# Moving the beginnings of the weight tiles by 16 to 240 bytes in a decoder trunk

## The chip, the cores and the metric

The kernel runs on one core of a Trainium2 chip. The metric is the device time of one execution in microseconds; several executions are timed, and one more is taken by the hardware profiler, whose records are read below.

## What is computed

A causal trunk of two decoder layers on 512 tokens of width 1024, in fp32. Layer 0 mixes tokens by multi-scale retention (4 heads), layer 1 by forgetting attention (16 heads). All is laid out with features on partitions and tokens along the columns.

```python
for i in range(DEPTH):                                   # 2 layers
    h = h + 0.5 * swiglu(rmsnorm(h, nw[0]), ffn_w_in[i, 0], ffn_w_out[i, 0])   # 1024 -> 2 x 2816 -> 1024
    hn = rmsnorm(h, nw[1])
    h = h + (retention(hn, ...) if i % 2 == 0 else forgetting_attention(hn, ...))
    h = h + 0.5 * swiglu(rmsnorm(h, nw[2]), ffn_w_in[i, 1], ffn_w_out[i, 1])
    gate = jax.nn.sigmoid(rmsnorm(h, nw[3]) @ ple_w_gate[i])
    h = h + gate * (p[i] @ ple_w_proj[i])
return rmsnorm(h, final_norm_w)
```

## The kernel before

Every product is made with fp32r operands that are split in two: a high part (the value rounded to fp32r) and a low part (the rest). Three matmuls stand for one: high x high, high x low, low x high (`mm3`, L310 to L314). A matmul takes 128 x 128 weights, which TensorE loads before it (PEld in the profile), and a moving operand of 128 rows and 128, 256 or 512 columns.

**Moving operands.** The activations lie in *units*, tiles of 128 x 512 fp32 (2,048 bytes a partition), in the pools `ua`, `ub`, `uc` and `ud`. A matmul moves a whole unit (512 columns) or a half (256).

**Weights.** The class `Weights` brings every weight tile in the order of a list, `W.plan`, two tiles ahead of use. `load` starts a DMA of 128 x 1024 fp32 into a `wraw` tile on SyncE's queue; `split` (L82, L83) lets ScalarE write the high part and VectorE or GpSimd the low part into a tile of the name `w8`, 128 x 2 x 1024, which the profile calls `w`; `negated` (L120 to L122) makes the low part with ScalarE and an adding DMA from GpSimd's queue. `w8` tiles come from `wpool`, three in turn; in the last stage from `wkept` with five, and two more of its weight tiles are put into units of `ub`. Three functions make a `w8` tile: `chunk`, `emit_parts` (the first two tiles of the program) and `first` (a `Pair`).

**Where the tiles meet which columns.**

- The four FFNs. Two blocks of the 22 are made in a plain way (`plain`, L524, 256 columns, 96 matmuls a block). The other 20 are *pairs* in a Strassen-like scheme: `product` (L493) makes 12 matmuls of 256 columns, and a pair has seven such products, two with the `w8` tile (`pair.t`), five with sums of the quarters of the weights, which VectorE adds up (L151) and which lie in tiles `s12`, `s34` and `a12` (`s` and `a` in the profile) of a pool that is opened for one FFN. So 24 of 84 matmuls of a pair have `w8` weights.
- The FFNs' second matrix (`out_blocks`, L312 to L314): 512 columns, in three parts of 6, 8 and 8 blocks of the activations. In each part the first two of the eight output blocks are made in turn, three matmuls with the one tile, three with the other.
- The projections of both mixers, the output projections and the first gated embedding (`proj`, `out_part`, `OutBoth`, `ple`): 512 columns, L312 to L314. In `v_part` (L678 to L680) it is the other way round: units are the weights, and the `w8` tile moves with 512 columns.
- The last gated embedding works on two halves of the tokens: 256 columns, L312 to L314.

**Where the tiles lie.** The pools follow one another along each partition. The units, `wraw` and `wpool` hold tiles whose lengths are multiples of 2,048 bytes, so all units and all `w8` tiles of `wpool` begin at the same place modulo 256. The distance of a tile from this place, modulo 256, is called its *beginning* here: 0 for units and these `w8` tiles. Every piece of weights within a tile lies a multiple of 512 bytes behind its start, so it has the tile's beginning. The pool `stat` behind them holds six small tiles that take 32 bytes each, and so whatever pool is opened later begins 192 bytes further: the tiles `s12`, `s34`, `a12` and the five of `wkept` have the beginning 192.

The order of TensorE's instructions is written by hand (`manual_schedule`); the other engines run in the order of issue.

Of the kernel before, what the change touches and what calls it, by code (L numbers as in the profile page):

```python
# [12 lines left out]
F32R = mybir.dt.float32r  # L13
# [4 lines left out]
P = 128  # L18
# [7 lines left out]
RH = 4  # L26
FH = 16
LOOKAHEAD = 2
KEPT = 7
PLAIN = (2, 2, 2, 2)  # L30
CHUNKS = [((0, 6), (6, 14), (14, 22)) for n in PLAIN]
# [4 lines left out]
class Pair:  # L36
# [3 lines left out]
    def __init__(self, ffn, q, r):  # L40
        self.ffn, self.q, self.r, self.direct = ffn, q, r, False
# [13 lines left out]
class Weights:  # L55
# [3 lines left out]
    def __init__(self, tc, raw_pool, pool):  # L59
        self.tc, self.nc, self.raw_pool, self.pool = tc, tc.nc, raw_pool, pool  # L60
        self.plan, self.ready, self.used = [], [], 0
        self.low = self.nc.vector
        self.limit, self.spare = None, []
        self.sum_pool, self.open_ffn, self.pairs_used = None, None, 0
        self.ahead, self.behind = 0, ()

    def emit(self, upto):
        while len(self.ready) < min(upto, self.limit):
            src = self.plan[len(self.ready)]
            self.ready.append(self.first(src) if isinstance(src, Pair) else self.chunk(src))  # L70
            self.emit_sums()

    def load(self, src):
        raw = self.raw_pool.tile([P, 1024], F32, name="wraw")
        self.nc.sync.dma_start(out=raw[:, : src.shape[1]], in_=src)
        return raw

    def split(self, raw, hi, lo, src=None):
        if self.low is None and src is not None:
            self.negated(raw, hi, lo, src)  # L80
            return
        self.nc.scalar.copy(hi, raw)  # L82
        self.low.tensor_tensor(out=lo, in0=raw, in1=hi.bitcast(F32), op=ALU.subtract)  # L83

    def chunk(self, src):
        n = src.shape[1]
        raw = self.load(src)
        if self.spare:
            tiles = [self.spare.pop(0)() for _ in range(4)]
            for i in range(2):  # L90
                self.split(raw[:, 512 * i : 512 * (i + 1)], tiles[i], tiles[2 + i])
            return Halves(tiles[0:2]), Halves(tiles[2:4])
        t = self.pool.tile([P, 2, 1024], F32R, name="w8")
        self.split(raw[:, :n], t[:, 0, :n], t[:, 1, :n], src)
        return t[:, 0, :], t[:, 1, :]

    def emit_parts(self, parts):

        nc = self.nc
        halves = lambda ap: ap.rearrange("p (h c) -> p h c", h=2)  # L100
        tiles = [
            (
                self.raw_pool.tile([P, 1024], F32, name="wraw"),
                self.pool.tile([P, 2, 1024], F32R, name="w8"),
            )
            for _ in range(2)
        ]
        for j0, j1 in parts:
            cs = slice(j0 * P, j1 * P)
            for src, (raw, t) in zip(self.plan, tiles):  # L110
                r, hi, lo = (halves(x)[:, :, cs] for x in (raw, t[:, 0, :], t[:, 1, :]))
                nc.sync.dma_start(out=r, in_=halves(src)[:, :, cs])
                nc.vector.tensor_copy(hi, r)
                nc.vector.tensor_tensor(out=lo, in0=r, in1=hi.bitcast(F32), op=ALU.subtract)
            yield
        self.ready += [(t[:, 0, :], t[:, 1, :]) for _, t in tiles]
# [7 lines left out]
    def first(self, pair):  # L124

        pair.raw = self.load(pair.q)
        pair.t = self.pool.tile([P, 2, 1024], F32R, name="w8")
        hi, lo = pair.t[:, 0, :], pair.t[:, 1, :]
        if pair.direct:
            self.split(pair.raw, hi, lo)  # L130
        else:
            self.negated(pair.raw, hi, lo, pair.q)
# [41 lines left out]
    def take(self, src):  # L174
        assert self.plan[self.used] is src
        self.emit(self.used + 1 + LOOKAHEAD)
        self.used += 1
# [10 lines left out]
def trunk(ctx, tc, a):  # L188
# [9 lines left out]
    wraw = ctx.enter_context(tc.tile_pool(name="wraw", bufs=4))  # L198
    wpool = ctx.enter_context(tc.tile_pool(name="wpool", bufs=LOOKAHEAD + 1))
    tmp = ctx.enter_context(tc.tile_pool(name="tmp", bufs=7))  # L200
# [4 lines left out]
    W = Weights(tc, wraw, wpool)  # L205

    def unit(pool):
        return pool.tile([P, S], F32R, name="unit_" + {id(ua): "a", id(ub): "b", id(uc): "c", id(ud): "d"}[id(pool)])


    ffn_src = []
    for i in range(4):
        ins = [Pair(i, a["ffn_w_in"][i, m, 0], a["ffn_w_in"][i, m, 1]) for m in range(NF)]
# [12 lines left out]
    ple_g = [[a["ple_gate"][l, m] for m in range(KB)] for l in range(2)]  # L226
    ple_p = [[a["ple_proj"][l, c] for c in range(2)] for l in range(2)]
# [11 lines left out]
    def plan_ple(l):  # L239
        W.plan += [ple_p[l][0]] + ple_g[l][0:5] + [ple_p[l][1]] + ple_g[l][5:8]  # L240
# [22 lines left out]
    plan_ffn(3)  # L263
    plan_ple(1)
    W.limit = len(W.plan) - KEPT


    hall = hpool.tile([P, KB, S], F32, name="hall")
# [42 lines left out]
    def mm3(out, wh, wl, xh, xl, first, last):  # L311
        nc.tensor.matmul(out, wh, xh, start=first, stop=False)  # L312
        nc.tensor.matmul(out, wh, xl, start=False, stop=False)  # L313
        nc.tensor.matmul(out, wl, xh, start=False, stop=last)  # L314
# [749 lines left out]
    def ple(l, n, nxt, phi, plo, parts=1):  # L1064

        w = S // parts
        with ExitStack() as pools:
            if parts > 1:
                W.emit(W.limit)
                W.pool = pools.enter_context(tc.tile_pool(name="wkept", bufs=KEPT - 2, reuse_waits="tile"))  # L1070
                W.spare = [lambda: unit(ub)] * 8
# [120 lines left out]
    norms[2].extra = ud  # L1192
    first = W.emit_parts(((0, 1), (1, 2), (2, 4)))
    next(first)
    load_x(1, 2)
    load_x(2, 4)
# [15 lines left out]
    def ffn_ple(i, l, n, mid, nxt, stack, apool, parts):  # L1212
        phi, plo = [], []

        def load():
            pv = a["pT"][l].rearrange("(b p) t -> b p t", p=P)
            for b in range(2):
                t1 = temp()
                nc.sync.dma_start(out=t1, in_=pv[b])
                phi.append(unit(uc))  # L1220
                plo.append(unit(uc))
                split(t1, phi[b], plo[b])

        ffn(i, n, mid, stack, apool, load)
        stack = open_ffn(i + 1) if i < 3 else None
        ple(l, mid, nxt, phi, plo, parts)
        return stack
# [101 lines left out]
```

## Time and profile before

| | us |
|---|---|
| median of 3 runs | 2216.24 (2215.52 to 2218.65) |
| the profiled execution | 2215.98 |
| its span | 2214.2 |
| TensorE busy, matmuls (PE) | 2148.7 |
| TensorE busy, weight loads (PEld) | 1933.3 |
| VectorE busy (DVE) | 1459.4 |
| ScalarE busy (ACT) | 1203.1 |
| GpSimd busy (POOL) | 466.8 |

The mean granted clock of TensorE was 0.99. A row of a group reads: line, engine, operation, out<-in by the program's names without buffer numbers (of a matmul the moving operand and the weights), shape, count, then busy us, the mean of one in ns, and the idle time before them with what ended it. A matmul's recorded duration includes the way through TensorE's pipeline, and the next one starts before it ends; how fast matmuls follow one another is read from their starts in the timeline. There a row merges equal instructions that follow one another: start, length in us, and their count at the end.

### The profile page before, as it was taken

What the parts mean: (1) busy time and instruction counts of PE and PEld (TensorE: products, weight loads), DVE (VectorE), ACT (ScalarE), POOL (GpSimd) and SP (SyncE); (2) the same over time, 40 slices, a digit from 0 to 9 for tenths busy, and PEclk for the clock granted to TensorE, in tenths of its full rate; (3) what the DMA queues carried; (4) which work ended last, traced back from release to release, by engine and by line L of the source; (5) the groups of instructions that cost most, each with busy time, mean ns of one, the idle gap of its engine ahead of it and who ended that gap; (6) DMA issues with size and microseconds to landing.
All of it is one profiled execution on the core that took longest, in us unless ns stands there. A gap on an engine that the chain in (4) does not pass through costs nothing.

```text
span 2214.2 us, 34442 instructions
## 1 busy us (share of the span) xinstructions
PE 2148.7 (97%) x13525; PEld 1933.3 (87%) x13525; DVE 1459.4 (66%) x2631; ACT 1203.1 (54%) x2027; POOL 466.8 (21%) x352
## 2 busy tenths in 40 slices
PE   7999999999999999999998999999999999999997
PEld 7999997888888798989887989898788898999987
DVE  8687776352533677867758677675575686777764
ACT  7565453343333564746545646364786775554643
POOL 0011013444344000101142001012243200110154
PEclk9999999999999999999999999999999999999999
DMA  5465562222222244645523456373622234655631
GB/s 174 111 168 150 141 163 95 74 94 81 94 78 86 77 126 128 167 126 149 144 92 97 117 142 178 117 166 102 154 86 86 77 112 113 162 155 142 156 105 39
DMA packets 85315, 267.08 MB, mean 121 GB/s; under 512 B 9360, under 2 KB 12944, under 8 KB 85152
## 3 DMA queue, kind: packets, MB, share of 16 engines
q1 hardware_dynamic: 63328, 209.78, 28.0%
q0 software_dynamic: 20592, 54.01, 14.4%
q8 instruction: 106, 1.74, 0.3%
q10 hardware_dynamic: 1232, 1.09, 0.1%
q14 instruction: 57, 0.47, 0.1%
HBM read 262.71 MB, written 2.13 MB: 120 GB/s over the span
## 4 chain that ended last, share of the span: by engine, by line
PE 81%; DVE 7%; ACT 5%; issue 4%; DMA 3%; POOL 1%; SPq 0%; DVEq 0%; ACTq 0%; POOLq 0%
PE bank L493 31%; PE bank L314 13%; PE bank L312 13%; PE bank L313 13%; PE bank L524 3%; DMA wraw<-in_ffn_w_in 2%; PE bank L678 2%; PE bank L679 2%; PE bank L680 2%; DVE w L83 1%; POOL w L83 1%; ACT p L982 1%; ACT w L82 1%; DVE sums L151 1%; DVE tlo L303 1%
## 5 line engine op out<-in xcount | busy, mean ns | idle before, releaser
L82 ACT CAST w<-wraw 128x1024 fp32r<-128x1024 f32 (+1 forms) x242 | 245.5, 1022 | 439.7 <-PE bank L314 257.3
L314 PE MATMUL bank<-unit_a,w 128*128 128x512 f32 x736 | 287.9, 391 | 4.3 <-DVE w L83 2.6
L312 PE MATMUL bank<-unit_a,w 128*128 128x512 f32 x736 | 289.2, 393 | 1.9 <-ACT w L82 1.6
L313 PE MATMUL bank<-unit_a,w 128*128 128x512 f32 x736 | 287.2, 390 | 0.2 <-DVE unit_a L303 0.2
L83 POOL TENSOR_TENSOR w<-wraw,w 128x1024 fp32r<-128x1024 f32 x93 | 226.5, 2439 | 273.7 <-ACT w L82 259.6
L314 PE MATMUL bank<-unit_d,w 128*128 128x512 f32 (+1 forms) x712 | 267.8, 376 | 4.7 <-DVE w L83 4.7
L312 PE MATMUL bank<-unit_d,w 128*128 128x512 f32 (+1 forms) x712 | 268.9, 378 | 3.3 <-ACT w L82 1.6
L82 ACT CAST s<-sums 128x512 fp32r<-128x512 f32 x320 | 191.1, 617 | 146.6 <-DVE sums L151 100.8
L313 PE MATMUL bank<-unit_d,w 128*128 128x512 f32 (+1 forms) x712 | 268.0, 376 | 1.7 <-DVE unit_d L303 1.7
L83 DVE TENSOR_TENSOR s<-sums,s 128x512 fp32r<-128x512 f32 x320 | 213.8, 686 | 83.1 <-ACT s L82 82.0
L122 POOL DMA_DIRECT2D a<-in_ffn_w_in x80 | 70.3, 878 | 654.4 <-ACT a L121 448.0
L83 DVE TENSOR_TENSOR w<-wraw,w 128x1024 fp32r<-128x1024 f32 (+1 forms) x149 | 175.8, 1185 | 23.4 <-ACT w L82 23.3
L493 PE MATMUL bank<-unit_b,s 128*128 128x256 f32 x880 | 185.4, 277 | 0.0
L493 PE MATMUL bank<-unit_d,s 128*128 128x256 f32 x1140 | 178.3, 276 | 0.0
L493 PE MATMUL bank<-unit_a,s 128*128 128x256 f32 x1260 | 176.1, 277 | 1.9 <-ACT unit_a L376 1.1
L585 DVE SCALAR_TENSOR_TENSOR tmp<-bank,rows 128x512 f32<-128x512 f32 x96 | 66.1, 690 | 166.3 <-PE bank L314 165.1
L314 PEld LDWEIGHTS bank<-unit_a,w 128*128 128x128 f32 x736 | 138.5, 188 | 35.7 <-DVE w L83 4.4
L312 PEld LDWEIGHTS bank<-unit_a,w 128*128 128x128 f32 x736 | 138.6, 188 | 32.3 <-ACT w L82 3.5
L313 PEld LDWEIGHTS bank<-unit_a,w 128*128 128x128 f32 x736 | 138.7, 188 | 28.7 <-DVE unit_a L303 0.5
L493 PEld LDWEIGHTS bank<-unit_a,s 128*128 128x128 f32 x1260 | 158.8, 188 | 2.7 <-ACT unit_a L376 1.6
L314 PEld LDWEIGHTS bank<-unit_d,w 128*128 128x128 f32 x712 | 134.1, 188 | 30.8 <-DVE w L83 6.6
L312 PEld LDWEIGHTS bank<-unit_d,w 128*128 128x128 f32 x712 | 134.1, 188 | 30.1 <-ACT w L82 3.3
(268 smaller groups left out, 4780.1 us busy)
## 6 DMA issues: line engine op xcount, KB each, us to landing
wraw<-in_ffn_w_in SPq DMA_DIRECT2D x174, 512.0 KB, 4.3
wraw<-in_ffn_w_out SPq DMA_DIRECT2D x64, 512.0 KB, 4.7
w<-in_ffn_w_in POOLq DMA_DIRECT2D x56, 512.0 KB, 5.3
a<-in_ffn_w_in POOLq DMA_DIRECT2D x80, 256.0 KB, 6.2
wraw<-in_ffn_w_out SPq DMA_DIRECT2D x32, 384.0 KB, 3.5
wraw<-in_ret_qk SPq DMA_DIRECT2D x16, 512.0 KB, 3.5
wraw<-in_ret_v SPq DMA_DIRECT2D x16, 512.0 KB, 3.6
wraw<-in_ret_g SPq DMA_DIRECT2D x16, 512.0 KB, 3.4
```

What stands on the lines that cost most here:

```text
L82: self.nc.scalar.copy(hi, raw)
L83: self.low.tensor_tensor(out=lo, in0=raw, in1=hi.bitcast(F32), op=ALU.subtract)
L122: self.nc.gpsimd.dma_start(out=lo, in_=src, accum_op=ALU.add)
L312: nc.tensor.matmul(out, wh, xh, start=first, stop=False)
L313: nc.tensor.matmul(out, wh, xl, start=False, stop=False)
L314: nc.tensor.matmul(out, wl, xh, start=False, stop=last)
L493: add = lambda w, x, start, stop: nc.tensor.matmul(out, w, x, start=start, stop=stop, skip_group_check=True)
L524: nc.tensor.matmul(o[:, HALVES[t]], x[:, ks], y, start=k == t == q == 0, stop=k == KB - 1 and q == 2, skip_group_check=True,)
L585: nc.vector.scalar_tensor_tensor(out=t1, in0=o, scalar=-0.5, in1=n.r, op0=ALU.mult, op1=ALU.mult)
L678: nc.tensor.matmul(os[t], xh, wh[:, js], start=k == 0, stop=False)
L679: nc.tensor.matmul(os[t], xh, wl[:, js], start=False, stop=False)
L680: nc.tensor.matmul(os[t], xl, wh[:, js], start=False, stop=k == KB - 1)
```

## The change

A `w8` tile is made 256 bytes longer (2,112 instead of 2,048 fp32 a partition), and the 2,048 that are used begin somewhat later in it: 192 bytes (48 elements) for the weights named in `narrow`, those of the FFNs' first matrices and of the last gated embedding; for all others at one of nine places, 16, 128, 144, 160, 176, 192, 208, 224 or 240 bytes, which follow one another tile by tile. High and low part of a tile, 4,096 bytes apart, have the same beginning.

```diff
+PLACES = (4, 32, 36, 40, 44, 48, 52, 56, 60)
...
+        self.narrow, self.turn = set(), 0
...
+    def wide(self, src):
+
+        at = 48
+        if id(src) not in self.narrow:
+            at = PLACES[self.turn % len(PLACES)]
+            self.turn += 1
+        t = self.pool.tile([P, 2112], F32R, name="w8")
+        return t[:, at : at + 2048].rearrange("p (a c) -> p a c", a=2)
...
-        t = self.pool.tile([P, 2, 1024], F32R, name="w8")
+        t = self.wide(src)
...
-                self.pool.tile([P, 2, 1024], F32R, name="w8"),
+                self.wide(src),
...
-        pair.t = self.pool.tile([P, 2, 1024], F32R, name="w8")
+        pair.t = self.wide(pair.q)
...
+    for ins, _ in ffn_src:
+        W.narrow |= {id(x) for pair in ins for x in (pair.q, pair.r)}
+    W.narrow |= {id(x) for x in ple_g[1] + ple_p[1]}
```

The three tiles of `wpool` together grow by 768 bytes, three times 256, so `stat` and all pools behind it keep their places modulo 256: the `s12`, `s34` and `a12` tiles still begin at 192. The tiles of `wkept`, which began at 192 already, have their used part at 384, which is 128 modulo 256. The units that stand in for two weight tiles of the last stage stay at 0.

More of the change, by code (lines that the diff above doesn't have):

```diff
@@ L103, in emit_parts @@
                 self.raw_pool.tile([P, 1024], F32, name="wraw"),
-                self.pool.tile([P, 2, 1024], F32R, name="w8"),
+                self.wide(src),
             )
-            for _ in range(2)
+            for src in self.plan[:2]
         ]
```

## The prediction

> **What bounds the kernel now.** I read the page first: the head with the busy times, then the chain of work that ended last, then the groups by line with shapes kept apart.
>
> ```profile
> span 2214.2 us, 34442 instructions
> PE 2148.7 (97%) x13525; PEld 1933.3 (87%) x13525; DVE 1459.4 (66%) x2631; ACT 1203.1 (54%) x2027; POOL 466.8 (21%) x352
> ...
> PE 81%; DVE 7%; ACT 5%; issue 4%; DMA 3%; POOL 1%; SPq 0%; DVEq 0%; ACTq 0%; POOLq 0%
> ```
>
> TensorE is busy in 2148.7 of 2214.2 us, so all its idle time is 65.5 us, and the chain puts 81% of the span on it. What a matmul takes is therefore what the kernel takes. The profiled execution took 2215.98 us, 0.26 below the median of 2216.24, so the sum below starts from 2216.0.
>
> The groups show that matmuls of one shape do not all take the same time. The columns are line, engine, operation, out<-moving,weights, shape, count, then busy us and mean ns of one.
>
> ```profile
> L493 PE MATMUL bank<-unit_b,s 128*128 128x256 f32 x880 | 185.4, 277 | 0.0
> L493 PE MATMUL bank<-unit_b,w 128*128 128x256 f32 x720 | 132.8, 284 | 8.7 <-ACT tmp L545 8.7
> L493 PE MATMUL bank<-unit_d,w 128*128 128x256 f32 x540 | 90.0, 283 | 0.0
> L493 PE MATMUL bank<-unit_a,w 128*128 128x256 f32 x540 | 82.2, 288 | 5.5 <-ACT tmp L545 5.5
> L493 PE MATMUL bank<-unit_c,w 128*128 128x256 f32 x120 | 27.4, 283 | 0.0
> ...
> L524 PE MATMUL bank<-unit_b,w 128*128 128x256 f32 x244 | 40.1, 309 | 11.3 <-ACT w L82 5.7 <-POOL w L83 2.4 <-DVE w L83 2.1
> ```
>
> With weights from an `s` tile one takes 277 ns, with weights from a `w8` tile (here `w`) 283 to 288, although both multiply 128x128 by 128x256. These times contain the pipeline's tail; what counts is the spacing of the starts, and that stands in the timeline of TensorE in the middle of the first FFN:
>
> ```profile
> 147.68 2.88 PE L493 MATMUL bank<-unit_a,s 128*128 128x256 f32 x24
> 150.40 1.60 PE L493 MATMUL bank<-unit_a,w 128*128 128x256 f32 x12
> 151.84 0.73 PE L493 MATMUL bank<-unit_b,s 128*128 128x256 f32 x5
> ```
>
> 24 matmuls with `s` weights fill 150.40 - 147.68 = 2.72 us, 113.3 ns each. The 12 with `w8` weights that follow, on the same moving tiles, fill 1.44 us, 120.0 ns each. What differs is where the weights lie: as the pools are laid out, an `s` tile begins 192 bytes past the phase of the moving unit tiles (counted modulo 256), and a `w8` tile begins in exactly their phase. So 6.7 ns per matmul hang together with the beginning, and the change gives `w8` tiles that meet 256 columns the beginning of the `s` tiles.
>
> The Trainium skill speaks against this reading: SBUF — State Buffer, section "Who interferes with whom", says that only VectorE and GpSimd share a port pair and that "PE and ACT never wait on anyone", and TensorE: Matmul & The Clock Gate, Part 2, gives the weight load a read port of its own. By that rule no beginning matters. The two spacings above, 113.3 and 120.0 ns for one shape, do not agree with it, unless something else than the beginning sets them apart; that is the fourth rival below.
>
> **The change, part by part.**
>
> *Instructions.* None is added, removed or moved; on every engine the same rows stand in the same order. The nine-place turn is taken while the program is built. Nothing waits for anything new.
>
> *Tiles of 256 columns.* `product` (L493) uses a `w8` tile in 24 of the 84 matmuls of a pair, and there are 80 pairs: 1920, which is 720 + 540 + 540 + 120 of the rows above. `plain` (L524) is called 8 times with 96 matmuls: 768. If each goes from 120.0 to 113.3 ns, that is 1920 x 6.67 = 12.8 us and 768 x 6.67 = 5.1 us. Is it on the path? I asked for the busy time of each engine in one stretch of `product` work.
>
> ```profile
> 127.00:204.00 77.00, 77.00 (x671) 77.00 (x670) 63.48 (x114) 55.02 (x96) 11.37 (x13) 1.00 0.71 181
> ```
>
> The columns behind the length are PE, PEld, DVE, ACT, POOL, then clock and DMA share. TensorE never pauses there, VectorE works 63.48 of 77 us and ScalarE 55.02. A pair takes 84 matmuls, 24 x 120.0 + 60 x 113.3 = 9.68 us, and would take 9.52; VectorE's share would go from 82% to 84%. So I count the 12.8 us whole; if VectorE paced the stage after all, part of it would come back as waits in `three` and `finish`. In `plain` TensorE does wait: 11.3 us before the 244 matmuls of the row above, for weights that ScalarE, GpSimd and VectorE split. There a faster matmul partly waits longer, and I take three quarters of 5.1, 3.8 us. Together 16.6 us.
>
> *The last stage.* The five `w8` tiles of `wkept` lie behind the `stat` pool and so already begin 192 bytes on; with 192 more they begin 128 on (384 less 256). Their row of starts in the last stage, first and last of 20:
>
> ```profile
> 2168.33 0.28 PE L312 MATMUL bank<-unit_d,w 128*128 128x256 f32 x1
> ...
> 2170.57 0.28 PE L313 MATMUL bank<-unit_c,w 128*128 128x256 f32 x1
> ```
>
> 19 steps in 2.24 us are 117.9 ns. These weights begin 192 bytes past the phase of the moving tiles and yet take neither 113.3 nor 120.0 ns; the 240 matmuls with such weights may go to either, which is 240 x 4.6 down or 240 x 2.1 up, 1.1 or 0.5 us. The 144 others of this stage, with tiles of `wpool`, may gain 144 x 6.7 = 1.0 us. I count nothing for either.
>
> *Tiles of 512 columns.* 4680 matmuls: L312 to L314 with 736, 616 and 16 each, and `v_part` with 3 x (128 + 64), where the `w8` tile is the moving operand.
>
> ```profile
> L312 PE MATMUL bank<-unit_a,w 128*128 128x512 f32 x736 | 289.2, 393 | 1.9 <-ACT w L82 1.6 <-DVE tmp L1016 0.3
> L312 PE MATMUL bank<-unit_d,w 128*128 128x512 f32 x616 | 241.8, 392 | 3.3 <-ACT w L82 1.6 <-DVE unit_b L306 0.6 <-ACT unit_d L302 0.5
> L678 PE MATMUL bank<-w,unit_a 128*128 128x512 f32 x128 | 49.9, 390 | 0.0
> ```
>
> Their spacing, from two starts with 14 matmuls between them in an output part of the first FFN:
>
> ```profile
> 119.40 0.39 PE L312 MATMUL bank<-unit_d,w 128*128 128x512 f32 x1
> ...
> 122.80 0.39 PE L312 MATMUL bank<-unit_d,w 128*128 128x512 f32 x1
> ```
>
> 3.40 us over 15 steps are 226.7 ns, all at the same beginning, 0. No run of 512-column matmuls at another beginning is long enough in this trace to read a spacing, so I bound it. The lower bound applies the 6.7 ns that the beginning is worth at 256 columns: 220.0 ns, and 4680 x 6.7 = 31 us less. The upper bound is what this beginning itself gives just after a wait, in the same part:
>
> ```profile
> 103.05 0.39 PE L312 MATMUL bank<-unit_d,w 128*128 128x512 f32 x1
> ...
> 104.67 0.39 PE L313 MATMUL bank<-unit_d,w 128*128 128x512 f32 x1
> ```
>
> Seven steps in 1.62 us, 231.4 ns each, before the stream settles to 226.7. If it never settled at the new beginnings, that is 4680 x 4.7 = 22 us more; if every tile began with seven such steps, 4680 / 24 = 195 tiles x 33 ns = 6 us. I take 0, since 226.7 is twice 113.3 to the last digit: the rate of 512 columns at beginning 0 is already that of the best 256-column run, and a rate that two shapes share looks like what TensorE can draw at most.
>
> The Trainium skill, TensorE: Matmul & The Clock Gate, "Back-to-back issue gap", has N / 2.4 + 2.5 ns, 215.8 for 512 columns and 109.2 for 256; no run of this trace reaches either, and were it reached at the new beginnings, the estimate would be 4680 x 10.9 = 51 us less from the large tiles alone.
>
> *Other engines.* ScalarE, VectorE, GpSimd and the DMAs write the shifted tiles with the shapes they had. No row shows a write at a start that is odd in 16 bytes. Of the fox weights whose low part a DMA adds, TensorE waits for one, 1.7 us; the slowest split is GpSimd's:
>
> ```profile
> PE bank L679 <- DMA w<-in_fox_v: 1.7, 1, 1.7
> ```
>
> ```profile
> L83 POOL TENSOR_TENSOR w<-wraw,w 128x1024 fp32r<-128x1024 f32 x93 | 226.5, 2439 | 273.7 <-ACT w L82 259.6
> ```
>
> It takes 2.44 us for a tile on which TensorE works 24 x 0.227 = 5.4 us, so a split twice as slow would still be covered. I count 0 for all of these.
>
> Sum: 2216.0 - 12.8 - 3.8 = 2199.4, given as **2199**.
>
> **The rivals.**
>
> *The large tiles gain too.* For it: at 256 columns, beginning 0 is the worst that the trace shows (120.0, against 117.9 and 113.3), so it may not be the best at 512 either. Against it: the doubling. Price: up to another 31 us, of which I take 28, the rest lost to weights that come late: 2171.
>
> *The large tiles lose.* For it: 226.7 is reached after a settling of some seven matmuls, and with beginnings that change from tile to tile, two of them in turn in the first blocks of each output part, the settling may start again and again. `v_part` gets other phases again, as its moving side shifts. Price 6 to 22 us on top of -16.6: 2205 to 2222.
>
> *The 256-column stream falls into its slower pace; this one ends slower than before.* Behind a wait the trace shows `s` weights at another spacing, though nothing about their tiles differs:
>
> ```profile
> 60.87 1.57 PE L493 MATMUL bank<-unit_a,s 128*128 128x256 f32 x12
> 62.28 0.75 PE L493 MATMUL bank<-unit_b,a 128*128 128x256 f32 x5
> ```
>
> 12 matmuls in 1.41 us, 117.5 ns, as in the last stage, where no weights at beginning 0 come in between. A few matmuls later, after 12 with `w8` weights at beginning 0, the same kind of stream runs at 113.3. So the stream seems to have two paces at 192, and it may be just the `w8` tiles at 0, two runs of 12 in each pair, that bring it back to the fast one. The change takes them away. At 117.5 throughout, 2688 `w8` matmuls gain 2.5 ns each, 6.7 us, and the 4800 with `s` and `a` weights lose 4.2 each, 20.2 us: 13.5 us more, 2229. With a share f of the stream in the slow pace the change is -17.9 + 31.4 f us, so it decides from f = 0.57. Against it: the slow pace is rare before, and the parts with 512 columns, which lie between the stretches, may bring the stream back as well; the trace cannot say, since each stretch behind them is entered through a `w8` tile at 0.
>
> *The beginning does nothing.* Another difference between `s` and `w8` tiles (their row of 512 or 1024 columns, who wrote them) sets the spacing. For it: the 117.9 of the last stage at 192. Price 0: 2216.
>
> **How the numbers follow.** My forecast (256-column tiles fast, large ones unchanged, 2193 to 2206) gets 0.38; the large tiles gain too (2160 to 2193) 0.25; they lose 0.17, half of which is still faster than before; the slow pace 0.14, mostly with part of the stream in it, 2208 to 2230; nothing 0.06. Two runs of this kernel can be told apart from about 0.2%, 4.4 us: faster means below 2211.8, slower above 2220.7. Faster: 0.38 + 0.25 + 0.09 less a little for my not having seen any long run of these beginnings, 0.68. Same: 0.13, from nothing and the middle of the two losing cases. Slower: 0.19. The range of 8 in 10 runs from 2170, which leaves out the best of the second case, to 2223, which leaves out the full slow pace.
>
> **What the profile after would show.** Starts of `product` with `w8` weights 113.3 ns apart and those with `s` weights still at 113.3; the mean of the four L493 `w` groups 276 or 277 ns instead of 283 to 288; L312 to L314 with 512 columns still at 390 to 393. I am wrong if the `s` groups rise to 280 (slow pace), if the L312 groups move by more than 2 ns either way (large tiles), or if the `w` groups stay at 283 (nothing). If the groups fall and the span does not, the wait rows of TensorE will name who paces instead.

## The result, and the profile after

The changed kernel takes 2245.1 us (2243.28 to 2245.14, 4 runs) against 2215.88 us for the kernel before beside it: a ratio of 1.0132, 95% interval 1.0116 to 1.0148, 29 us slower. The forecast was 17 us faster.

The head of the page after:

```profile
span 2241.5 us, 34442 instructions
PE 2177.7 (97%) x13525; PEld 1944.8 (87%) x13525; DVE 1458.8 (65%) x2631; ACT 1203.1 (54%) x2027; POOL 467.4 (21%) x352
```

TensorE is busy 29.0 us longer (2177.7 against 2148.7), with as many instructions; its idle time is 63.8 us against 65.5. The other engines do what they did. So TensorE does not wait more: the matmuls themselves follow one another more slowly. The groups say which (L507 is L493 of before, L326 to L328 are L312 to L314, L692 is L678):

```profile
L326 PE MATMUL bank<-unit_a,w 128*128 128x512 f32 x736 | 291.7, 396 | 1.8 <-ACT w L93 1.5 <-DVE tmp L1030 0.3
...
L326 PE MATMUL bank<-unit_d,w 128*128 128x512 f32 x616 | 244.0, 396 | 3.2 <-ACT w L93 1.5 <-ACT unit_d L316 0.7 <-DVE unit_b L320 0.6
...
L507 PE MATMUL bank<-unit_b,s 128*128 128x256 f32 x880 | 188.5, 280 | 0.0
...
L507 PE MATMUL bank<-unit_b,w 128*128 128x256 f32 x720 | 131.6, 282 | 6.4 <-ACT tmp L559 6.4
...
L692 PE MATMUL bank<-w,unit_a 128*128 128x512 f32 x128 | 50.6, 396 | 0.0
```

The large matmuls rose from 393 to 396 ns (in `v_part` from 390 to 396), the `s` ones from 277 to 280; the `w` ones of L507 went from 283 to 288 down to 282 to 284. Summed over every interval from one start to the next, waits included, without the last 156 matmuls of the program, the 512-column matmuls take 1145.4 us against 1128.6 (16.8 more), the 256-column ones 988.3 against 976.8 (11.5 more). The spacings behind that, from the timeline after, in the same place of the first FFN:

```profile
147.38 2.99 PE L507 MATMUL bank<-unit_a,s 128*128 128x256 f32 x24
150.20 1.57 PE L507 MATMUL bank<-unit_a,w 128*128 128x256 f32 x12
151.62 0.75 PE L507 MATMUL bank<-unit_b,s 128*128 128x256 f32 x5
```

24 with `s` weights now fill 2.82 us, 117.5 ns each; before it was 113.3. The 12 with `w8` weights fill 1.42 us, 118.3 each; before 120.0. Over the whole trace the matmuls of `product` and `plain` average 117.3 ns with `s` and `a` weights (before 113.4) and 117.1 with `w8` weights (before 119.9), intervals above 130 ns left out.

At 512 columns a tile at beginning 160 and one at 240, each with 12 steps between its two rows:

```profile
231.20 0.40 PE L326 MATMUL bank<-unit_d,w 128*128 128x512 f32 x1
...
234.00 0.40 PE L326 MATMUL bank<-unit_d,w 128*128 128x512 f32 x1
```

```profile
503.61 0.39 PE L327 MATMUL bank<-unit_d,w 128*128 128x512 f32 x1
...
506.33 0.39 PE L327 MATMUL bank<-unit_d,w 128*128 128x512 f32 x1
```

At 160 it is 2.80 / 12 = 233.3 ns, at 240 2.72 / 12 = 226.7, which before was the spacing of nearly every large tile.

### The profile page after: what moved, and what is told of

Its sections match the earlier page's. It is cut to its first block, busy times and chain, and to the rows that moved or that the text cites. A ratio compares the mean times of both kernels' runs of the same rounds, so it can differ in the third digit from the quotient of the medians.

```text
span 2241.5 us, 34442 instructions
## 1 busy us (share of the span) xinstructions
PE 2177.7 (97%) x13525; PEld 1944.8 (87%) x13525; DVE 1458.8 (65%) x2631; ACT 1203.1 (54%) x2027; POOL 467.4 (21%) x352
## 3 DMA queue, kind: packets, MB, share of 16 engines
q0 software_dynamic: 20592, 54.01, 14.2%
## 4 chain that ended last, share of the span: by engine, by line
PE 85%; DVE 7%; ACT 4%; issue 2%; DMA 1%; POOL 0%; SPq 0%; DVEq 0%; ACTq 0%; POOLq 0%
PE bank L507 32%; PE bank L328 14%; PE bank L326 14%; PE bank L327 14%; PE bank L538 3%; PE bank L692 2%; PE bank L693 2%; PE bank L694 2%; DVE w L94 1%; ACT w L93 1%; DMA wraw<-in_ffn_w_in 1%; DVE sums L162 1%; ACT p L996 1%; DVE tlo L317 1%; DVE hall L1125 1%
## 5 line engine op out<-in xcount | busy, mean ns | idle before, releaser
L328 PE MATMUL bank<-unit_a,w 128*128 128x512 f32 x736 | 289.8, 394 | 4.4 <-DVE w L94 2.7
L326 PE MATMUL bank<-unit_a,w 128*128 128x512 f32 x736 | 291.7, 396 | 1.8 <-ACT w L93 1.5
L94 POOL TENSOR_TENSOR w<-wraw,w 128x1024 fp32r<-128x1024 f32 x93 | 227.1, 2445 | 278.7 <-ACT w L93 266.1
L328 PE MATMUL bank<-unit_d,w 128*128 128x512 f32 (+1 forms) x712 | 269.8, 379 | 4.7 <-DVE w L94 4.7
L326 PE MATMUL bank<-unit_d,w 128*128 128x512 f32 (+1 forms) x712 | 271.2, 381 | 3.2 <-ACT w L93 1.5
L507 PE MATMUL bank<-unit_b,s 128*128 128x256 f32 x880 | 188.5, 280 | 0.0
L507 PE MATMUL bank<-unit_d,s 128*128 128x256 f32 x1140 | 183.4, 279 | 0.0
L507 PE MATMUL bank<-unit_a,s 128*128 128x256 f32 x1260 | 180.0, 279 | 1.8 <-ACT unit_a L390 1.1
L328 PEld LDWEIGHTS bank<-unit_a,w 128*128 128x128 f32 x736 | 138.3, 188 | 38.6 <-DVE w L94 4.4
L326 PEld LDWEIGHTS bank<-unit_a,w 128*128 128x128 f32 x736 | 138.3, 188 | 34.6 <-ACT w L93 3.5
L507 PEld LDWEIGHTS bank<-unit_a,s 128*128 128x128 f32 x1260 | 162.1, 188 | 2.6 <-ACT unit_a L390 1.6
L328 PEld LDWEIGHTS bank<-unit_d,w 128*128 128x128 f32 x712 | 133.8, 188 | 33.3 <-DVE w L94 6.6
L326 PEld LDWEIGHTS bank<-unit_d,w 128*128 128x128 f32 x712 | 133.9, 188 | 32.2 <-ACT w L93 3.3
```

The costliest lines, as they stand in the source:

```text
L507: add = lambda w, x, start, stop: nc.tensor.matmul(out, w, x, start=start, stop=stop, skip_group_check=True)
```

## The experiments

Ten kernels. "Before" in a ratio is the kernel before on the same chip. Unless the text says so, a kernel is the changed one with the lines shown replaced; all compute the whole function. Where an expectation multiplies matmuls by "us", as in "4800 x 3.9 us", the factor is in ns.

**The two halves apart.** First only the 256-column tiles moved:

```diff
-PLACES = (4, 32, 36, 40, 44, 48, 52, 56, 60)
+PLACES = (0,)
```

> Only the 256-column tiles moved, to 192 bytes; all others stay at beginning 0. Slow-pace theory (the 256-column stream at 192 has a fast and a slow pace, and the tiles at 0 used to bring it back to the fast one): the s and w8 groups of L493 stay near the 117.3 ns of the changed kernel, the 512-column ones at 227; 4800 x 3.9 us up, 2826 x 2.8 down, about 11 us slower than before, 2227. Rival (the slow pace comes in from the odd beginnings of the 512-column tiles that run before): with those back at 0 the stream is entered in the fast pace, 113.4 everywhere, 17 us faster than before, 2199.

Measured: 2229.05 us, ratio 1.0045 (1.0032 to 1.0059), TensorE busy 2160.8 us, 12.1 more than before.

```profile
L326 PE MATMUL bank<-unit_a,w 128*128 128x512 f32 x736 | 288.4, 392 | 1.9 <-ACT w L93 1.6 <-DVE tmp L1030 0.3
...
L507 PE MATMUL bank<-unit_b,s 128*128 128x256 f32 x880 | 188.3, 280 | 0.0
```

The large ones are back at 392 ns, the `s` ones stay at 280. So the slow pace of the 256-column stream needs no help from the moved 512-column tiles; the rival falls.

This pair of kernels also shows where the fast pace came from. Both enter the stream out of the same output part, with large tiles at 0; first before, then this run:

```profile
126.88 0.88 PE L493 MATMUL bank<-unit_b,w 128*128 128x256 f32 x6
...
128.32 2.88 PE L493 MATMUL bank<-unit_a,s 128*128 128x256 f32 x24
131.04 1.60 PE L493 MATMUL bank<-unit_a,w 128*128 128x256 f32 x12
```

```profile
126.89 0.87 PE L507 MATMUL bank<-unit_b,w 128*128 128x256 f32 x6
...
128.31 2.99 PE L507 MATMUL bank<-unit_a,s 128*128 128x256 f32 x24
131.13 1.58 PE L507 MATMUL bank<-unit_a,w 128*128 128x256 f32 x12
```

Behind 12 matmuls with the `w8` tile at 0 the first `s` run takes 2.72 / 24 = 113.3 ns, behind the same 12 at 192 2.82 / 24 = 117.5. It is so at all 11 places where the stream is entered from an output part or from `plain` (the first stretch of the program left out): before, the `s` run behind the first `w8` tile is fast at all 11, here slow at all 11. Then only the other tiles:

```diff
-        at = 48
+        at = 0
```

> Only the other tiles moved, over the nine beginnings; the 256-column ones are at 0 as before. Theory of two separate losses: 256 columns back at 113.4 (s) and 119.9 (w8), 512 columns at 231.9 as in the changed kernel, 17 us slower than before, 2233. Rival (the loss at 512 columns is a late effect of the 256-column stream): 512 columns at 227, no change, 2216.

Measured: 2233.79 us, ratio 1.0060 (1.0043 to 1.0078), TensorE busy 2167.1 us, 18.4 more than before.

```profile
L326 PE MATMUL bank<-unit_a,w 128*128 128x512 f32 x736 | 291.7, 396 | 1.8 <-ACT w L93 1.5 <-DVE tmp L1030 0.3
...
L507 PE MATMUL bank<-unit_b,s 128*128 128x256 f32 x880 | 185.4, 277 | 0.0
```

Now `s` is back at 277 and the large ones stay at 396. The two losses are separate, and their busy times add up: 12.1 + 18.4 = 30.5 us, against the 29.0 of the whole change. The device times do so less well: 0.45% and 0.60% make 1.05%, against 1.32% for the whole; the uncertainties (0.14, 0.17 and 0.16 points either way) leave room for both sums.

**Large tiles: the turn, or the beginnings?** All 512-column tiles at 160, the 256-column ones at 0:

```diff
-PLACES = (4, 32, 36, 40, 44, 48, 52, 56, 60)
+PLACES = (40,)
...
-        at = 48
+        at = 0
```

> The 512-column tiles all at one beginning, 160 bytes, where the changed kernel shows 233.7 ns for each; the 256-column ones at 0. Own-pace theory (each beginning has its own lasting pace, whatever came before): 4104 x 6.5 and 576 x 6.5 us up, 30 us slower than before, 2246. Rival (the loss comes from changing the beginning from tile to tile, and a single one would settle): 512 columns settle to 227, 2216 to 2220.

Measured: 2237.85 us, ratio 1.0079 (1.0064 to 1.0095). Nothing changes from tile to tile here, and yet nothing settles to 227: of 119 tiles with 24 matmuls in a row, 116 run at 233.3 ns in their second half. Nine steps of one of them, 2.10 us:

```profile
340.23 0.39 PE L326 MATMUL bank<-unit_d,w 128*128 128x512 f32 x1
...
342.33 0.39 PE L326 MATMUL bank<-unit_d,w 128*128 128x512 f32 x1
```

TensorE's busy time rises by 25.6 us, near the expected 30; the execution lost less, 17.5 us by the ratio, since part of it only filled TensorE's waits (61.7 us of idle time instead of 65.5) and executions differ by some us in how long the clock is halved (in the profile of before the granted clock is 0.50 from 53.8 to 60.4 us; over a whole execution it is 0.987 to 0.992 among the runs of before).

The same with all at 240, where the changed kernel had shown the old spacing (`PLACES = (60,)`, `at = 0`):

> All 512-column tiles at the one beginning 240, the 256-column ones at 0. The changed kernel shows 226.7 or 228.3 ns there, depending on how the stream enters. Own-pace theory: 512 columns at 227 to 228.5, 0 to 6 us slower than before, 2218 to 2224. Rival (any move away from 0 costs): 232, 20 us slower. The second rival, that 512 columns can go below 226.7 at some beginning, would show here at the latest as a spacing of 220.

Measured: 2220.56 us, ratio 1.0013 (0.9998 to 1.0027).

```profile
L326 PE MATMUL bank<-unit_a,w 128*128 128x512 f32 x736 | 289.4, 393 | 1.9 <-ACT w L93 1.6 <-DVE tmp L1030 0.3
```

84 of 119 tiles run at 226.7, 33 at 228.3, `v_part` (beginning 16 from its moving side) at 233.8. The three `w8` buffers lie 8,448 bytes apart, 33 times 256, and by the order in which tiles take turns in them all three show both spacings (226.7 in 27, 27 and 31 tiles), so the place modulo 256 is what shows. Moving away from 0 costs next to nothing in itself; the beginning counts. The seven beginnings that are not among the nine places:

```diff
-PLACES = (4, 32, 36, 40, 44, 48, 52, 56, 60)
+PLACES = (0, 8, 12, 16, 20, 24, 28)
...
-        at = 48
+        at = 0
```

> The 512-column tiles take turns over 0 and the six beginnings that the nine places leave out, 32 to 112 bytes; the 256-column ones are at 0. Theory that 226.7 ns is the least that 512 columns can take: no beginning shows a lasting spacing below 226.7, most show 228 to 234, the time is 5 to 20 us above before. Rival (there are faster beginnings, the nine places are just not among them): one of the six shows 220 or less.

Measured, one execution: 2233.12 us, against 2219.38 for before. With the changed kernel's own nine this gives all sixteen, as the mean spacing in the second half of tiles with 24 matmuls in a row:

```
beginning, bytes   ns per matmul of 512 columns (tiles)
0                  226.7 (17 of 17 here, 113 of 117 in the kernel before)
16                 226.7 (10 of 16) or 233.3 (5)
32, 48, 64, 112    233.3 (all but one of 68)
80                 232.0
96                 234.1
128                232.6
144, 160, 224      233.3 (37 of 39)
176                230.0 (12 of 12)
192                228.9 (10 of 12)
208                231.5 to 233.3
240                226.7 (10 of 14) or 228.3 (4)
```

None is below 226.7. The rival of faster large tiles falls: with every tile at 0 the kernel before stood at the best of the sixteen. The Trainium skill, TensorE: Matmul & The Clock Gate, "Back-to-back issue gap", has 215.8 ns (N / 2.4 + 2.5) for an isolated matmul of this size at full clock; no beginning gives it in these streams, and the measurement decides.

**256 columns: is it the beginning at all?** The kernel before, with only the `s` and `a` tiles moved, by 64 bytes to 0, by a function that makes `pair.s` and `pair.x`:

```diff
+    def sums_tile(self, name, bufs):
+        t = self.sum_pool.tile([P, 1088], F32R, name=name, bufs=bufs)
+        return t[:, 16 : 16 + 1024].rearrange("p (a c) -> p a c", a=2)
```

> The kernel before, but its s and a tiles begin at 0 instead of 192, as its w8 tiles do. If the beginning sets the pace and not the kind of tile, all 256-column matmuls of the FFNs take 120.0 ns: 4800 x 6.6 us more than before, 32 us slower, 2250. Rival (s tiles are faster for another reason, their shorter rows or who writes them): s stays at 113.4, no change, 2218.

Measured: 2242.46 us, ratio 1.0114 (1.0093 to 1.0135), TensorE busy 2175.2 us, 26.5 more. That is less than the 32 expected; the wait for ScalarE's copy of a sum fell from 14.2 to 11.4 us, and the rest is not accounted for.

```profile
159.59 3.04 PE L497 MATMUL bank<-unit_a,s 128*128 128x256 f32 x24
162.47 0.76 PE L497 MATMUL bank<-unit_a,w 128*128 128x256 f32 x5
```

2.88 us for 24 are 120.0 ns: with the beginning of the `w8` tiles the `s` tiles have their spacing, to the digit. It is the beginning, not the kind of tile. The Trainium skill, SBUF — State Buffer, "Who interferes with whom", says that TensorE never waits on anyone; the prediction's conclusion from it, that no beginning matters, does not hold for these runs, though nothing here shows the reads or writes of another engine holding it up.

**One beginning or two.** The 256-column tiles took turns over all sixteen:

```diff
-PLACES = (4, 32, 36, 40, 44, 48, 52, 56, 60)
+PLACES = (0,)
+SURVEY = tuple(range(0, 64, 4))
...
-        at = 48
+        at = SURVEY[self.other % len(SURVEY)]
+        if id(src) in self.narrow:
+            self.other += 1
```

> The 256-column tiles take turns over all 16 beginnings by 16 bytes, the others stay at 0: a survey of the pace for each. If 0 alone brings the stream with s weights back to its fast pace, the s runs behind a tile at 0 take 113.3 ns and those behind all other tiles stay mixed or at 117.5; if any change of the beginning does it, most s runs take 113.3 and only those behind a tile at 192 can stay slow. The w8 runs themselves: 120.0 at 0; if the distance of the beginnings is what counts, some others reach 113.3 too. Total between 2205 and 2230.

Measured, one execution: 2229.86 us, against 2219.1 for before. The `s` and `a` runs average 117.3 ns; both theories that I had put down fall. The `w8` runs themselves take 120.0 to 120.4 ns at 0, 112 and 160, and between 116.4 and 119.8 at the other beginnings but 64. All 8 runs at beginning 0 that came from the slow pace ran at 120 and left the `s` run behind them slow. So a tile at 0 does not always restore the fast pace, though before it gave it at every entry. Two others stood out: the first run of a pair at 240 left the stream fast in 6 of 6, and the second at 64 ran at 113.3 itself and left it fast in 4 of 4. At all other beginnings a stream that came slow was left slow, though there too the `s` tiles around it lay at 192. From that, `w8` at 64 with the rest unmoved (`PLACES = (0,)`, `at = 16`):

> The w8 tiles that meet 256 columns begin at 64, the s and a tiles stay at 192, the 512-column tiles at 0. In the survey the runs at 64 took 113.3 ns wherever the stream came to them from a 512-column part, and in the second run of a pair always, and the s runs behind were then fast. Theory that the pace is a state which the stream keeps: it is entered fast behind each output part and stays fast, 113.4 for s and for w8, 18 us faster than before, 2200. Rival (64 is fast only when it comes from the slow pace of s): the w8 runs mixed, s between 113.4 and 117.5, 2210 to 2228.

Measured: 2210.64 us, ratio 0.9963 (0.9947 to 0.9978): 8 us faster than the kernel before.

```profile
146.49 2.88 PE L507 MATMUL bank<-unit_a,s 128*128 128x256 f32 x24
149.21 1.52 PE L507 MATMUL bank<-unit_a,w 128*128 128x256 f32 x12
150.57 0.62 PE L507 MATMUL bank<-unit_b,s 128*128 128x256 f32 x4
```

TensorE's longest wait, in this kernel and in the kernel before (us in total, times, longest):

```profile
PE bank L507 <- ACT tmp L559: 20.1, 8, 5.6
```

```profile
PE bank L493 <- ACT tmp L545: 14.2, 6, 5.5
```

In the timeline both kinds run at 113.3: 2.72 / 24 and 1.36 / 12. Over the trace `w8` averages 114.4 and `s` 113.7. The gain is less than the 18 us hoped for, and two things are missing: all 8 stretches behind an output part were entered slow, against the expectation, and became fast only some products later (the 3 behind `plain` were fast at once); and this wait, for ScalarE's copy of a sum (L559 is L545 of before), rose from 14.2 to 20.1 us. Was it 64 as such? `s`, `a` and `w8` all at 64 (the `sums_tile` above at 32 elements instead of 16, `PLACES = (0,)` and `at = 16`):

> All 256-column tiles of the FFNs, s, a and w8, begin at 64; 512 columns at 0. If 64 has a fast pace that lasts, all take 113.3 ns and the time is 18 us below before, 2200. If a single beginning always ends in the slow pace, as 192 alone does (117.5), the time is 11 us above before, 2229.

Measured: 2224.57 us, ratio 1.0028 (1.0006 to 1.0051).

```profile
146.60 2.99 PE L511 MATMUL bank<-unit_a,s 128*128 128x256 f32 x24
149.43 1.58 PE L511 MATMUL bank<-unit_a,w 128*128 128x256 f32 x12
150.84 0.75 PE L511 MATMUL bank<-unit_b,s 128*128 128x256 f32 x5
```

Slow again: 2.83 / 24 = 117.9 and 1.41 / 12 = 117.5. And the two swapped, `w8` at 192 and the sums at 64 (as the last, but with `at = 48`):

> The run with the tiles at 64 and 192, swapped: w8 at 192, s and a at 64, 512 columns at 0. Theory that going to and fro between two beginnings brings the stream out of its slow pace, while a single one (192 throughout: 117.4, 64 throughout: 117.1) keeps it in: s and w8 fast in most runs, 113.5 to 114.6 on average, 5 to 10 us faster than before, 2207 to 2212. Rival (the fast pace hangs on which product uses which beginning, so that the swap loses it): 117 for both, 2224 to 2229.

Measured: 2213.24 us, ratio 0.9964 (0.9947 to 0.9981), as good as the run it mirrors.

```profile
146.88 2.88 PE L511 MATMUL bank<-unit_a,s 128*128 128x256 f32 x24
149.60 1.52 PE L511 MATMUL bank<-unit_a,w 128*128 128x256 f32 x12
150.96 0.28 PE L511 MATMUL bank<-unit_b,s 128*128 128x256 f32 x1
```

So neither 64 nor 192 is fast or slow by itself: with either alone the stream has both paces and keeps the one that it was entered with, and to and fro between the two it is led to the fast one. Counted in the one profiled execution of each kernel over runs of 12 matmuls with `w8` weights inside the stream, by the `s` or `a` run ahead and the `s` run behind (a run is fast if its last six starts lie under 114.3 ns apart on average; places with a longer wait or with the clock halved are left out, as the pace can change there):

```
beginning w8 / s     the run ahead slow: the s run behind fast   the run ahead fast: the s run behind fast
192 / 192            0 of 131                                    9 of 9
 64 / 64             0 of 121                                    18 of 18
 64 / 192            13 of 15                                    124 of 124
192 / 64             4 of 4                                      134 of 134
  0 / 192 (before)   3 of 4                                      137 of 137
```

## Why the prediction was wrong

**What bounds the kernel** was right: TensorE's own pace. Its busy time explains the whole loss, and no wait row changed by more than a few us.

**Tiles of 256 columns: the step that failed is "if each goes from 120.0 to 113.3 ns".** I took 113.3 for a property of the beginning 192. It is one of two paces that the stream can have there, and which one it has is carried along from matmul to matmul. The quoted rows of the last stage, 117.9 ns at 192, and of 60.87, 117.5 ns with `s` weights, showed the other pace, and I put them into a rival. That rival was right in its price: 13.5 us more if all ran at 117.5; the 256-column intervals grew by 11.5, and the half alone cost 10 us by its ratio. On the cause it was right in the main: the `w8` tiles at 0 gave the fast pace at all 11 entries before, and at 192 they gave it at none. That a tile at 0 brings back a slow stream held inside the stretches in 3 of 4 cases before and in none of the survey's 8. What is shown is that 192 alone and 64 alone keep whichever pace the stream has and never restored the fast one (0 of 131, 0 of 121), and that 64 and 192 in alternation keep it and mostly restore it (13 of 15, 4 of 4); for most other beginnings in alternation with 192 the survey shows no restoring.

**Tiles of 512 columns: the step that failed is "I take 0".** Its ground, that 226.7 is the most TensorE can draw, is not contradicted: nothing below it was found at any of sixteen beginnings. But a floor at 0 says only that other beginnings cannot gain; it does not say that they cost nothing. They cost up to 7 ns, lastingly. The rival had the right bounds, 6 to 22 us (16.8 measured), from the wrong mechanism: it is not a settling that starts again with every tile (160 alone, never changed, is slow in its second halves too), but a pace that belongs to the beginning. That the sum fell inside those bounds is in part luck: five of the nine beginnings run above the 231.4 that the upper bound was made from, and 176, 192, 240 and most tiles at 16, which run below it, made up for them.

**The range.** I gave the two losing rivals chances as if only one could come. Each came without the other when its half was run alone, one at 256 columns and one at 512, and in the whole change both came: 11.5 + 16.8 = 28.3 us. With the ends that I had, 13.5 + 22 = 35.5 above 2216, the range would have held the result.

**Other engines and the last stage** came out as counted: VectorE, ScalarE and GpSimd kept their busy times, GpSimd's split of a tile took 2445 ns against 2439, the matmuls with `wkept` tiles 118.6 ns against 117.8.

**What stays open.** What in the reading of weights and moving operand makes the beginning matter, and what carries the pace from matmul to matmul, is not visible in a trace of starts and ends. No run moved the units, so whether the distance between the two counts or the address of each is open; that the spacing also changes in `v_part`, where the moving side is what moves, shows only that it is not the weights' address alone. No run changed the other engines' work by itself; but at beginning 0 the large tiles run at 226.7 both from 330 to 700 us, where VectorE is busy 46% of the time, and, in 25 of 27 tiles, from 1560 to 1800 us, where it is busy 68%. Why a stretch behind an output part is entered slow with 64 and fast with 0 was not pursued, nor was the last stage tuned.

## What to carry to other kernels

Back-to-back matmuls of one shape can run at several lasting paces, and here the place of the weights modulo 256 bytes, counted from the moving operand's, had a part in deciding between them, together with what the stream did before: read spacings from the starts in the timeline by tile, not from mean durations, before and after any change that moves buffers, even one that only makes a pool longer. A pace seen behind one neighbour is not a property of the tile; ask what the stream did before it, and test a beginning in the whole pattern. When two rivals act on different instructions, add their prices for the range instead of choosing between them.

## What the runs showed of the hardware that was not expected

- At 256 columns and full clock: 113.3, about 117.5 or 120.0 ns; at 512 columns 226.7, 228.3, 228.9, 230.0 or 233.3 and some between, for the same instructions and data, as the weights' address moves in steps of 16 bytes (and, at 256 columns, by what ran before). The slowest pace is 6% above the fastest at 256 and 3% at 512.
- The best pace at 512 columns is twice the best at 256 to the digits shown, and the sixteen beginnings of the large tiles go no lower.
- A pace can last for a whole stretch: with 192 alone 131 of 131 runs that came slow left slow, 9 of 9 that came fast left fast. What decides it can be the first 12 matmuls: at 0 they led into the fast pace at 11 of 11 entries, at 192 at none of 11.
- Two kernels that set the 256-column tiles at 64 and 192 bytes, 128 apart, either way round, beat the kernel before by 0.37% (0.22 to 0.53) and 0.36% (0.19 to 0.53).
